# Spreading a memory's reciprocal norms over the partitions: matmuls of ones with a diagonal, or a DMA round trip over DRAM

## The chip, the core and the metric

The kernel runs on one core of one Trainium2 chip. The metric is device microseconds of one execution, the lower the better. The core has TensorE (PE in the profile; its weight loads are PEld), VectorE (DVE), ScalarE (ACT), GpSimd (POOL) and SyncE (SP), which issues nearly all DMAs; each engine runs its own queue of instructions in order.

## The reference, cut to what matters

The program is four blocks on 256 tokens of width 1024: an attention layer with global, windowed and memory heads, a layer with neighborhood and memory heads, a mixer, and a cross attention followed by a squared-ReLU MLP. Two of them read a memory, a [256, 1024] tensor that is normalised per token and projected to keys and values:

```python
memn = rmsnorm(mem, mem_norm_gain)
...
mk, mv = jnp.split(memn @ w_mem_kv[l], 2, axis=-1)
...
s = jnp.einsum('bshd,bmhd->bhsm', q, mk).astype(jnp.float32) * (dm ** -0.5)
...
kv = mem_n @ w_kv_mem
k, v = jnp.split(kv, 2, axis=-1)
```

The norm's factor is one number r per memory token. The kernel leaves it out of the projections and multiplies it in afterwards. Values come out with tokens on partitions, so r is a [128, 2] column there; keys come out transposed, with tokens along the free axis, so r is wanted as a [128, 256] tile that is alike in every partition.

## The kernel before, in words

Every weight matrix is streamed from DRAM in loads of up to 1 MB into one of three buffers of the tag `raw` (`load`, line 408). ScalarE copies a half of a load to `wh`, VectorE subtracts that from the load to get `wl` (`split`, line 413), and TensorE multiplies with three matmuls per product (hi by hi, hi by lo, lo by hi). A `raw` buffer is free once both of its halves are split. PSUM has two tags of four banks: `mm` for projections and `at` for everything of attention (`psum`, line 317). The softmax exponentials read the scores straight from their `at` bank (`softmax`, line 703), so a bank comes free only when ScalarE has run them. Attention steps are queued as background work between the pieces of weights (`later`, `pace`).

The order on each engine is not the order of the source. `Plan` (line 30) records all operations, takes a modelled cost for each (`cost`, line 131) and lists them by start with a list scheduler (`order`, line 162); then they are issued in that order, fixed, on each engine. Among the modelled figures: a POOL `pow` on [128, 2] takes 630 ns, and a DMA that isn't a weight load also waits, in the plan, for the matmul recorded before it (line 109).

`memory` (line 546) prepares a memory in background steps: squares of the two halves (`t_memraw`), then `finish`: `rstd` (line 500: one VectorE addition, one POOL `pow`), a VectorE copy to `t_memr`, and `spread` (line 491). It is called twice, for `mem` in the first layer and for `mem_2` in the second. `spread` writes the 256 numbers to DRAM (`t_rd`) and reads them back for all 128 partitions (`t_rb`), both on SyncE's queue, in which the weight loads stand too:

```python
nc.sync.dma_start(d.rearrange("(t p) -> p t", p=P), r)
b = self.base.tile([P, S], F32, name=self.name("rb"))
nc.sync.dma_start(b, d.rearrange("(o s) -> o s", o=1).to_broadcast([P, S]))
```

The only reader of `t_rb` is `mem_key` (line 577), which scales the keys. `layer_even` (line 954) already needs such a tile for the first input norm and makes it without DRAM (lines 982 to 988): VectorE scales the identity's columns by r to a diagonal, TensorE multiplies a [128, 128] tile of ones with it into an `at` bank, ScalarE copies the bank to SBUF.

Of the kernel before, what the change touches and what calls it, by code (L numbers as in the profile page):

```python
# [10 lines left out]
F32 = mybir.dt.float32  # L11
# [5 lines left out]
P = 128  # L17
S = 256
# [11 lines left out]
class Plan:  # L30
    """Records the program as operations on stand-ins of the tiles, then issues them in an order that keeps every
    dependence and the number of buffers of each tag, and that a list scheduler finds from the engines' costs."""
# [30 lines left out]
    def box(self, v):  # L63
        """the tile, the range of partitions and the set of elements in a partition, as bits, of an access"""
        t = self.tiles[v.tensor.name]
        if t["pool"].space == bass.MemoryType.DRAM:
            return t, (0, 1, 1)
        p0, f0 = divmod(v.offset, t["row"])
        if t["pool"].space == bass.MemoryType.PSUM:
            return t, (p0, p0 + v.ap[0][1], 1)  # L70
        bits = 1
        for step, num in sorted(list(v.ap)[1:], key=lambda d: abs(d[0])):
            if step < 0:
                f0 += step * (num - 1)
            if abs(step) == 1 and bits == 1:
                bits = (1 << num) - 1
            elif step:
                one = bits
                for k in range(1, num):
                    bits |= one << (abs(step) * k)  # L80
        return t, (p0, p0 + v.ap[0][1], bits << f0)
# [33 lines left out]
    def either(self, first, second):  # L115
        """an operation that one of two engines may run: each an engine, a method, its arguments and keywords"""
        self.record(*first)
        op = self.ops[-1]
        engine, method, args, kwargs = second
        out = args[0] if args else kwargs["out"]  # L120
        op["forms"].append((engine, method, args, kwargs, self.cost(engine, method, args, kwargs, [out], [args[1] if args else kwargs["in0"]])[0]))
        for j in op["deps"]:
            op["deps"][j] = max(op["deps"][j], self.latency(self.ops[j]["engine"], engine))
# [7 lines left out]
    def cost(self, engine, method, args, kwargs, outs, ins):  # L131
        """ns that the engine is held, ns until the result is there after that, bytes of a DMA"""
# [28 lines left out]
    # ------------------------------------------------------------------ order  # L161
    def order(self, prio):
        """a schedule: the operations by start, their starts and ends, and who held each back"""
# [104 lines left out]
    # ------------------------------------------------------------------ issue  # L268
# [18 lines left out]
class Kernel:  # L287
# [38 lines left out]
    # ------------------------------------------------- attention steps between the pieces of weights  # L326
# [18 lines left out]
    # ---------------------------------------------------------------- constants  # L345
# [61 lines left out]
    # ---------------------------------------------------------------- weights  # L407
# [19 lines left out]
    def proj_t(self, w, c0, hT, n=256, tag="mm"):  # L427
        """n (128 or 256) columns of h @ w, transposed: [128 columns, n / 128, 256 tokens] in one bank"""
        raw = self.load(w, 0, KT, c0, n)
        po = self.psum(tag)  # L430
        for f in range(n // P):
            wh, wl = self.split(raw[:, :, f * P:(f + 1) * P])
            for k in range(KT):
                self.mm3(po[:, f, :], wh[:, k, :], wl[:, k, :], hT(0, k), hT(1, k), k == 0, k == KT - 1)
                if k % 4 == 3:
                    self.pace()
        return po[:, :n // P, :]

    def proj_n(self, pieces, nk, n, hT, banks=None, start=True, stop=True):
        """h @ w for n columns in natural layout, a bank per token tile; pieces yields (first k tile, raw view)"""  # L440
# [16 lines left out]
    def wide(self, w, r0, nk, c0, n=512, step=4):  # L457
        """pieces of nk k-tiles by n columns, for proj_n; step k-tiles to a load"""
# [6 lines left out]
    # ---------------------------------------------------------------- norms  # L465
    def square_sums(self, src, c, ms):
        """ms[:, c, t] = the part of half c, src [P, 2, 512], in the mean of the squares over D"""
        for t in range(2):
            self.square_sum(src[:, t, :], ms[:, c, t:t + 1])

    def load_t(self, src, name):
        """[D, S] -> two tiles of 4 k-tiles"""
# [5 lines left out]
    def gain_t(self, src, key):  # L478
        """hi and lo of the tiles src with the gain: f(l, k) -> [P, S], and the step that fills k"""
# [11 lines left out]
    def spread(self, r):  # L491
        """[P, 2] per token -> [P, S], alike in every partition"""
        nc = self.nc
        d = self.dr.tile([S], F32, name=self.name("rd"))
        nc.sync.dma_start(d.rearrange("(t p) -> p t", p=P), r)
        b = self.base.tile([P, S], F32, name=self.name("rb"))
        nc.sync.dma_start(b, d.rearrange("(o s) -> o s", o=1).to_broadcast([P, S]))
        return b

    def rstd(self, ms):  # L500
        """ms [P, 2 parts, 2] -> [P, 2]"""
# [6 lines left out]
    def norm_twice(self, tag, gain, key, idle):  # L508
        """x = rmsnorm(x) * gain, and norm_later of that. Returns (after, go): after(c) for each half c of
        x once it is complete, then go() queues the steps and returns as turns"""  # L510
# [35 lines left out]
    def memory(self, tag, src, src_t, key, bias):  # L546
        """(src * gain).T, its hi and lo, and the rstd of src per token in both layouts, as attributes of a list
        filled in steps"""
# [12 lines left out]
        def finish():  # L561
            nc.vector.tensor_copy(r, self.rstd(ms))
            m[2] = self.spread(r)
# [13 lines left out]
    def mem_key(self, h, l, po, m):  # L577
        """hi and lo of po [P, 2, S] scaled per token"""
# [4 lines left out]
    def norm_later(self, tag, key, ms, idle):  # L583
        """rmsnorm(x).T in steps, the turning idle steps after the scaling"""
# [14 lines left out]
    def scaled(self, out, src, r):  # L599
        """out = src * r, r per partition"""  # L600
# [3 lines left out]
    def square_sum(self, v, ms):  # L604
        """ms = the part of v, [P, 512], in the mean of the squares over D"""
# [6 lines left out]
    def turns(self, tag, halves, key):  # L612
        """steps that fill hi and lo of (halves * gain).T; returns f(l, k) -> [P, S]"""
# [24 lines left out]
    # ---------------------------------------------------------------- evacuations  # L638
# [8 lines left out]
    def q_stack(self, po, scale):  # L647
        """[P, 2 pairs, S] of head pairs -> [P, 4 heads, S]; each head's rows hold its hi and lo parts"""
# [10 lines left out]
    def k_stack(self, po, pairs=2):  # L659
        """[P, pairs, S] of head pairs -> hi, lo [P, heads, S], both halves of the rows alike"""  # L660
# [15 lines left out]
    def v_heads(self, po):  # L676
        """two banks [P keys, 512] of 8 heads -> f(h)(k) -> [P, 128]: hi and lo of a head side by side"""
# [5 lines left out]
    # ---------------------------------------------------------------- attention  # L683
    def scores_stacked(self, q, kh, kl, spans):
        """spans: per query tile (first key, number of keys)"""
# [8 lines left out]
    def scores_full(self, parts):  # L694
        """parts: list of (qh, ql, kh, kl), each [P, S], summed over the list"""
# [7 lines left out]
    def softmax(self, sc, bias=None, sink=None, causal=False):  # L703
        """unnormalised weights and the reciprocals of their sums. With a bias, scores and bias are both
        negated."""
# [25 lines left out]
    def weights(self, p, rinv, causal=False):  # L731
        """normalised weights, transposed: hi, lo [P keys, 2, S queries]"""
# [16 lines left out]
    def pv_pair(self, ws, vs, causal=False):  # L749
        """o.T of two heads, [P, S]; vs: functions of the key tile giving a head's [P, 128] stationary, whose hi  # L750
        and lo columns give two halves of rows to be added"""
# [15 lines left out]
    def gate_tile(self, w, c0, hT):  # L767
        """2 * silu(h @ w[:, c0:c0+512]).T, [P, 4, S]"""
# [19 lines left out]
    def out_proj(self, w, r0, y, scale=None, after=None):  # L788
        """x += y @ w[r0:r0+512] (times a factor per token)"""
# [13 lines left out]
    def sums(self):  # L803
        """(ms, f): f(c) adds half c of x to ms once it is complete"""
# [10 lines left out]
    def filling(self):  # L815
        """projections of the second memory, as work for the tensor engine while it would wait"""
# [39 lines left out]
    def steps(self, tag, first, second, third, n, every):  # L856
        """queue the three steps of each of n heads, each step some steps behind the one before it; the third
        comes once for every heads"""
# [10 lines left out]
    def mem_heads(self, tag, qm, mk, mv, out):  # L869
        """steps of the four memory heads; out(h, o.T)"""  # L870
# [18 lines left out]
    def pair_heads(self, tag, n, scores, bias, sink, v, out, causal=False):  # L889
        """steps of n heads in pairs: scores(h), bias(h), sink(h), v(h)(l, k), out(pair, o.T)"""  # L890
# [14 lines left out]
    # ---------------------------------------------------------------- layers  # L905
    def rope(self, tag, po, n, i, rx):
        """steps of per-head rmsnorm and rotation of n heads of 64; po: a bank per token tile, still to be
        scaled by rx; returns the list that they fill"""
# [45 lines left out]
    def layer_even(self):  # L954
# [27 lines left out]
        diag = self.work("p", [P, 2, P], PB)  # L982
        pb = self.psum("at")
        rb = self.work("y", [P, S], YB)
        for t in range(2):
            nc.vector.tensor_scalar(diag[:, t, :], self.ident, r[:, t:t + 1], None, ALU.mult)
            nc.tensor.matmul(pb[:, 0, t * P:(t + 1) * P], self.ones, diag[:, t, :], start=True, stop=True)
        nc.scalar.copy(rb, pb[:, 0, :])
# [78 lines left out]
    def heads8(self, tag, w_in, cq, ck, cv, hT, bias, out, causal=False, before=None):  # L1067
        """8 heads of 64; the scores come out negated"""
# [76 lines left out]
    def token_rms(self, sq):  # L1145
        """sq [P, 4, S]: squares, of 4 feature tiles, over their number -> rstd [P, 2] per token"""
# [306 lines left out]
```

## Time and profile before

| what | before |
|---|---|
| time, median of 3 runs (lowest to highest) | 796.77 us (792.59 to 798.28) |
| profiled execution: span from first to last instruction | 790.9 us |
| profiled execution: its own time with what lies around the span | not reported |
| TensorE busy | 771.2 us of the span |
| VectorE, ScalarE, POOL busy | 576.7, 505.3, 74.4 us |
| moved by DMA | 140.85 MB, mean 178 GB/s |

Every operation is issued from one line of `Plan.issue`, so all rows carry L284 and are told apart by their tiles: `t_wh<-t_raw` is a split on ScalarE, `t_at<-t_ks,t_qs` are scores, `t_p<-t_at,t_st` an exponential, `t_mm<-t_gh,t_wh` a projection of a memory. A line of the waits gives the engine that stood, what released it, total us, times and the longest. The chain of waits is followed back from the last instruction, each step to what released it. An fp32 matmul shows as two records here.

### The profile page before, as it was taken

How to read it: one execution, taken by the hardware profiler on the slowest of the kernel's cores; microseconds unless marked ns; L12 is line 12 of the kernel's file. 1: busy time of each engine (PE TensorE's matmuls, PEld its weight loads, DVE VectorE, ACT ScalarE, POOL GpSimd, SP SyncE). 2: the span in 40 equal slices, each digit the busy share in tenths (PEclk: the TensorE clock that was granted, in tenths of full speed). 3: DMA queues.
4: the chain of work that ended last, by engine and by line, in shares of the span. 5: the costliest groups of instructions: out<-in, count | busy, mean ns of one | idle time of the engine just before them, and what ended most of it. 6: DMA issues, size and time to landing. Idle time of an engine off the chain costs nothing.

```text
span 790.9 us, 13554 instructions
## 1 busy us (share of the span) xinstructions
PE 771.2 (98%) x5312; PEld 716.6 (91%) x5312; DVE 576.7 (73%) x991; ACT 505.3 (64%) x926; POOL 74.4 (9%) x105
## 2 busy tenths in 40 slices
PE   8997999999999999999999999999999999999996
PEld 7797899889899989997999899899989999999985
DVE  6996987997768759879987788975667544545444
ACT  6784966875658559648786777475456654555452
POOL 0640000000001420232011100100000000000000
PEclk9999999999999999999999999999999999999999
DMA  7794546345558785684457735356434555565631
GB/s 229 253 319 149 169 136 220 126 142 163 183 168 275 193 189 167 187 226 146 147 166 196 224 115 163 123 188 227 152 128 161 183 189 186 187 195 179 201 119 53
DMA packets 110827, 140.85 MB, mean 178 GB/s; under 512 B 4355, under 2 KB 82371, under 8 KB 110764
## 3 DMA queue, kind: packets, MB, share of 16 engines
q1 hardware_dynamic: 105292, 131.90, 51.3%
q0 software_dynamic: 5472, 8.10, 4.8%
q8 instruction: 41, 0.67, 0.4%
q14 instruction: 22, 0.18, 0.1%
HBM read 135.25 MB, written 1.07 MB: 172 GB/s over the span
## 4 chain that ended last, share of the span: by engine, by line
PE 85%; DVE 5%; DMA 5%; POOL 2%; issue 2%; ACT 1%; SPq 0%; POOLq 0%; ACTq 0%; DVEq 0%
PE t_mm L284 63%; PE t_at L284 22%; DVE t_wl L284 2%; DMA t_rd<-t_memr 2%; DMA t_raw<-in_w_mem_kv_dram 1%; DMA t_raw<-in_w_out_odd_dram 1%; DVE t_y L284 1%; POOL t_rrs L284 1%; DVE t_p L284 1%; ACT t_wh L284 1%; POOL t_ks L284 1%; DMA t_raw<-in_w_in_even_dram 1%; DVE t_xs L284 0%; POOL t_rstd L284 0%; ACT t_p L284 0%
## 5 line engine op out<-in xcount | busy, mean ns | idle before, releaser
L284 DVE TENSOR_TENSOR t_wl<-t_raw,t_wh 128x1024 fp32r<-128x1024 f32 (+1 forms) x237 | 290.1, 1228 | 147.4 <-ACT t_wh L284 146.9
L284 ACT ACTIVATE t_wh<-t_raw 128x1024 fp32r<-128x1024 f32 (+1 forms) x237 | 248.9, 1054 | 207.0 <-PE t_mm L284 136.0
L284 PE MATMUL t_mm<-t_mT,t_wh 128*128 128x256 f32 x992 | 192.4, 287 | 0.0
L284 PEld LDWEIGHTS t_mm<-t_mT,t_wh 128*128 128x128 f32 x992 | 159.4, 191 | 0.4
L284 PE MATMUL t_mm<-t_mT,t_wl 128*128 128x256 f32 x496 | 141.1, 285 | 0.0
L284 PE MATMUL t_mm<-t_wh,t_yh 128*128 128x512 f32 x288 | 113.7, 395 | 0.0
L284 PE MATMUL t_mm<-t_wl,t_yh 128*128 128x512 f32 x288 | 113.6, 395 | 0.0
L284 PE MATMUL t_mm<-t_wh,t_yl 128*128 128x512 f32 x288 | 113.1, 394 | 0.0
L284 PE MATMUL t_at<-t_mT,t_wh 128*128 128x256 f32 x480 | 97.0, 282 | 0.0
L284 PEld LDWEIGHTS t_mm<-t_mT,t_wl 128*128 128x128 f32 x496 | 95.0, 192 | 0.0
L284 PEld LDWEIGHTS t_at<-t_mT,t_wh 128*128 128x128 f32 x480 | 78.8, 190 | 1.6
L284 PE MATMUL t_mm<-t_wh,t_gh 128*128 128x256 f32 (+2 forms) x256 | 66.0, 340 | 1.7 <-ACT t_wh L284 1.7
L284 PE MATMUL t_at<-t_mT,t_wl 128*128 128x256 f32 x240 | 67.6, 282 | 0.0
L284 PE MATMUL t_mm<-t_hT,t_wh 128*128 128x256 f32 x336 | 66.2, 287 | 0.2 <-ACT t_wh L284 0.2
L284 PEld LDWEIGHTS t_mm<-t_wh,t_yl 128*128 128x128 f32 x288 | 54.2, 188 | 10.7
L284 PEld LDWEIGHTS t_mm<-t_wl,t_yh 128*128 128x128 f32 x288 | 54.2, 188 | 10.0
L284 PEld LDWEIGHTS t_mm<-t_wh,t_yh 128*128 128x128 f32 x288 | 54.2, 188 | 9.7
L284 ACT ACTIVATE t_p<-t_p,t_st 128x256 f32<-128x256 f32 (+1 forms) x118 | 55.8, 490 | 7.6 <-DVE t_st L284 7.4
L284 POOL TENSOR_TENSOR t_rstd<-t_rstd,t_mhalf 128x2 f32<-128x2 f32 (+1 forms) x12 | 12.2, 1015 | 477.1 <-DVE t_rstd L284 477.1
L284 PEld LDWEIGHTS t_mm<-t_hT,t_wh 128*128 128x128 f32 x336 | 54.1, 191 | 0.5 <-ACT t_wh L284 0.4
L284 PE MATMUL t_mm<-t_gh,t_wh 128*128 128x256 f32 x256 | 51.6, 290 | 0.0
L284 PEld LDWEIGHTS t_mm<-t_wh,t_gh 128*128 128x128 f32 x256 | 44.6, 193 | 6.3 <-ACT t_wh L284 1.9
(171 smaller groups left out, 1318.0 us busy)
## 6 DMA issues: line engine op xcount, KB each, us to landing
t_raw<-in_w_in_odd_dram SPq DMA_DIRECT2D x20, 1024.0 KB, 5.2
t_raw<-in_w_up_dram SPq DMA_DIRECT2D x16, 1024.0 KB, 5.4
t_raw<-in_w_down_dram SPq DMA_DIRECT2D x16, 1024.0 KB, 4.9
t_raw<-in_w_in_dram SPq DMA_DIRECT2D x12, 1024.0 KB, 5.2
t_raw<-in_w_in_even_dram SPq DMA_DIRECT2D x10, 1024.0 KB, 5.0
t_raw<-in_w_mem_kv_dram SPq DMA_DIRECT2D x8, 1024.0 KB, 8.3
t_raw<-in_w_out_even_dram SPq DMA_DIRECT2D x6, 1024.0 KB, 5.0
t_raw<-in_w_out_odd_dram SPq DMA_DIRECT2D x6, 1024.0 KB, 5.8
```

What stands on the lines that cost most here:

```text
L284: f(*[self.real(v) for v in args], **{k: self.real(v) for k, v in kwargs.items()})
```

## The change

`spread` takes the tile to fill as an argument and makes it with the chain that `layer_even` had inline; `layer_even` calls it, with the same tiles as before, and `memory` calls it for both memories. The DRAM tile and the two DMAs per memory are gone. The plan is made anew from the changed list of operations. The rest of the diff empties docstrings and comments.

```diff
-    def spread(self, r):
...
-        nc = self.nc
-        d = self.dr.tile([S], F32, name=self.name("rd"))
-        nc.sync.dma_start(d.rearrange("(t p) -> p t", p=P), r)
-        b = self.base.tile([P, S], F32, name=self.name("rb"))
-        nc.sync.dma_start(b, d.rearrange("(o s) -> o s", o=1).to_broadcast([P, S]))
+    def spread(self, r, b):
+
+        nc = self.nc
+        diag = self.work("p", [P, 2, P], PB)
+        pb = self.psum("at")
+        for t in range(2):
+            nc.vector.tensor_scalar(diag[:, t, :], self.ident, r[:, t:t + 1], None, ALU.mult)
+            nc.tensor.matmul(pb[:, 0, t * P:(t + 1) * P], self.ones, diag[:, t, :], start=True, stop=True)
+        nc.scalar.copy(b, pb[:, 0, :])
         return b
...
             nc.vector.tensor_copy(r, self.rstd(ms))
-            m[2] = self.spread(r)
+            m[2] = self.spread(r, self.base.tile([P, S], F32, name=self.name("rb")))
...
         r = self.token_rms(sq[0])
-        diag = self.work("p", [P, 2, P], PB)
-        pb = self.psum("at")
-        rb = self.work("y", [P, S], YB)
-        for t in range(2):
-            nc.vector.tensor_scalar(diag[:, t, :], self.ident, r[:, t:t + 1], None, ALU.mult)
-            nc.tensor.matmul(pb[:, 0, t * P:(t + 1) * P], self.ones, diag[:, t, :], start=True, stop=True)
-        nc.scalar.copy(rb, pb[:, 0, :])
+        rb = self.spread(r, self.work("y", [P, S], YB))
```

## Rows read from the trace of the kernel before

**Rows 1.** The page, part 1 (busy time, share of the span and number of instructions of each engine) and the granted clock of TensorE in 40 equal slices of part 2.

```profile
PE 771.2 (98%) x5312; PEld 716.6 (91%) x5312; DVE 576.7 (73%) x991; ACT 505.3 (64%) x926; POOL 74.4 (9%) x105
...
PEclk9999999999999999999999999999999999999999
```

**Rows 2.** Who waited for whom, the waits of TensorE's own queue, longest first. Columns: engine and tile that waited, arrow, what released it, then us in total, times, longest us.

```profile
PE t_at L284 <- ACT t_p L284: 4.8, 1, 4.8
PE t_mm L284 <- ACT t_wh L284: 1.9, 2, 1.7
PE t_at L284 <- DVE t_st L284: 1.8, 1, 1.8
PE t_at L284 <- DVE t_p L284: 1.6, 3, 1.0
```

**Rows 3.** The chain of waits that ended last, in the stretch 44 to 84 us. Columns: start us, us, what.

```profile
59.98 11.10 DMA t_raw<-in_w_mem_kv_dram
...
71.16 1.06 ACT t_wh L284
72.22 1.83 ACT t_p L284 x8
...
74.09 1.22 PE t_at L284 x4
```

**Rows 4.** Instructions of TensorE in order of time, 64 to 83 us. Columns: start us, us, engine, line, operation, out<-in, shape, count, and in brackets the idle time before and its releaser.

```profile
69.05 0.28 PE L284 MATMUL t_mm<-t_gh,t_wh 128*128 128x256 f32 x1
74.09 1.22 PE L284 MATMUL t_at<-t_ks,t_qs 128*128 128x256 f32 x4 [4.76 <-ACT t_p L284]
```

**Rows 5.** Busy time of each engine (PE, PEld, DVE, ACT, POOL) in stretches of 2 us, then granted clock, share of the DMA engines and GB/s.

```profile
74.00:76.00 2.00, 1.91 (x9) 1.91 (x10) 2.00 (x5) 2.00 (x8) 0.00 (x0) 0.50 0.03 12
76.00:78.00 2.00, 2.00 (x14) 2.00 (x14) 2.00 (x3) 1.06 (x3) 0.00 (x0) 0.74 0.52 147
```

**Rows 6.** Issues on SyncE's queue in order of time, 18 to 100 us. Columns as in the group of TensorE's instructions above.

```profile
57.68 0.37 SPq L284 DMA_DIRECT2D t_rd<-t_memr  x1
59.98 0.37 SPq L284 DMA_DIRECT2D t_raw<-in_w_mem_kv_dram  x1
66.41 0.34 SPq L284 DMA_DIRECT2D t_rb<-t_rd  x1
```

**Rows 7.** DMA queues in the stretch 58 to 66.4 us: packets of all queues, then issues with size and us from issue to landing.

```profile
DMA packets 417, 0.23 MB, mean 28 GB/s; under 512 B 277, under 2 KB 346, under 8 KB 416
...
t_raw<-in_w_mem_kv_dram SPq DMA_DIRECT2D x1, 1024.0 KB, 11.1
t_rd<-t_memr SPq DMA_DIRECT2D x1, 1.0 KB, 8.7
```

**Rows 8.** The page, part 6, issues over the whole span. Columns: out<-in, queue, operation, count, KB each, median us to landing.

```profile
t_raw<-in_w_in_odd_dram SPq DMA_DIRECT2D x20, 1024.0 KB, 5.2
...
t_raw<-in_w_mem_kv_dram SPq DMA_DIRECT2D x8, 1024.0 KB, 8.3
...
t_raw<-in_w_out_odd_dram SPq DMA_DIRECT2D x6, 1024.0 KB, 5.8
```

**Rows 9.** Instructions of ScalarE in order of time, 50 to 86 us.

```profile
71.16 1.06 ACT L284 ACTIVATE t_wh<-t_raw 128x1024 fp32r<-128x1024 f32 x1 [6.79 <-DMA t_raw<-in_w_mem_kv_dram]
```

**Rows 10.** The chain of waits in the stretch 255 to 300 us.

```profile
267.92 12.49 DMA t_rd<-t_memr
...
280.87 8.36 DMA t_raw<-in_w_out_odd_dram
...
292.45 0.74 PE t_at L284 x4
```

**Rows 11.** SyncE's waits over the whole span, those on the first DMA of the round trip.

```profile
SPq L284 <- DMA t_rd<-t_memr: 17.9, 2, 11.9
```

**Rows 12.** Instructions of VectorE, 262 to 294 us.

```profile
271.77 1.23 DVE L284 TENSOR_TENSOR t_wl<-t_raw,t_wh 128x1024 fp32r<-128x1024 f32 x1 [1.49 <-ACT t_wh L284]
...
290.42 1.23 DVE L284 TENSOR_TENSOR t_wl<-t_raw,t_wh 128x1024 fp32r<-128x1024 f32 x1 [4.11 <-ACT t_wh L284]
```

**Rows 13.** Instructions of all engines in the first layer, 18 to 26 us, where the same chain of ones and diagonal already stands.

```profile
20.41 0.39 PE L284 MATMUL t_mm<-t_wh,t_gh 128*128 128x512 f32 x1
...
20.78 0.55 DVE L284 TENSOR_SCALAR t_p<-t_cst,t_rstd 128x128 f32<-128x128 f32 x2 [0.59 <-POOL t_rstd L284]
...
21.17 0.71 PE L284 MATMUL t_at<-t_p,t_ones 128*128 128x128 f32 x4 [0.37 <-DVE t_p L284]
...
21.64 0.48 PE L284 MATMUL t_mm<-t_wh,t_gh 128*128 128x512 f32 x1
...
22.14 0.36 ACT L284 COPY t_y<-t_at 128x256 f32<-128x256 f32 x1
```

**Rows 14.** VectorE's instructions around the two places, 50 to 86 us and then 244 to 254 us (two answers of one view).

```profile
55.57 0.16 DVE L284 SCALAR_TENSOR_TENSOR t_rstd<-t_ms 128x2 f32<-128x2 f32 x1
...
57.48 0.17 DVE L284 COPY t_memr<-t_rstd 128x2 f32<-128x2 f32 x1 [0.61 <-POOL t_rstd L284]
...
73.16 0.17 DVE L284 RECIPROCAL t_st<-t_st 128x2 f32<-128x2 f32 x1 [5.29 <-ACT t_p L284]
...
244.45 0.15 DVE L284 SCALAR_TENSOR_TENSOR t_rstd<-t_ms 128x2 f32<-128x2 f32 x1
...
250.04 0.16 DVE L284 COPY t_memr<-t_rstd 128x2 f32<-128x2 f32 x1
```

## The prediction

> **What bounds the kernel now.** I read the page's busy times first. TensorE is busy for 771.2 of 790.9 us, at nine tenths or more of the clock in every slice [rows 1], so a gain can only come from the 19.7 us in which it stands, or from its clock. Next come TensorE's own waits: the longest, 4.8 us, ends with an exponential on ScalarE, and another, 1.8 us, with a softmax statistic on VectorE [rows 2]. The chain of waits tells what was late behind each.
>
> At the first place the chain goes from a weight load of the memory's projections that took 11.10 us, over its split on ScalarE, over eight pieces of exponentials, to score matmuls at 74.09 [rows 3]. TensorE started its last projection matmul at 69.05 and stood for 4.76 us [rows 4], because the scores want an `at` bank, the bank comes free with an exponential, and ScalarE, whose queue has the split ahead of it, waited 6.79 us for the load [rows 9]. After that standstill the granted clock is 0.50 in 74 to 76 and 0.74 in 76 to 78 us [rows 5], that is time at 1.2 in place of 2.4 GHz. The load was issued at 59.98, behind the 1 KB write of the round trip (57.68), and SyncE came on only at 66.41 with the read back [rows 6]. That write took 8.7 us to land, and from 58 to 66.4 us all queues together moved 0.23 MB, 28 GB/s [rows 7]. So the 1 MB load stood behind a transfer of 1 KB on an otherwise nearly empty fabric.
>
> At the second place the chain names the write itself: 12.49 us, then a load of `w_out_odd` of 8.36 us, a split, scores at 292.45 [rows 10]. Here SyncE's queue was blocked: it waited 11.9 us for the write, 17.9 us over both places [rows 11].
>
> **Removed.** *First place.* Without the write, the load of 59.98 lands after the 5.2 us that loads of this size usually take [rows 8], at 65.2. Its split (1.06) and the exponentials (1.83) [rows 3] end at 68.1, before TensorE runs out at 69.3; the wait of 4.8 us goes. Bounds: loads of this one matrix have a median of 8.3 us [rows 8]; landing at 68.3, with the 3.0 us from landing to scores as now (71.08 to 74.09 [rows 3]), the scores would start at 71.3 and 2.0 of the wait would stay. I take 5.2, since what was in flight beside it is the write that goes. With the standstill goes the slow clock: 74.09 to 76 at half speed costs 0.95 us and 76 to 78 at 0.74 another 0.5 [rows 4, 5], together 1.5. What is late next is the second half of the keys' split, which VectorE does right after the exponentials; it has 2 to 3 us of other matmuls ahead of it. ScalarE's 6.79 us and VectorE's 5.29 us of idle time [rows 9, 14] go with TensorE's, so the attention work behind moves up by as much as TensorE does.
>
> A rule of the Trainium skill speaks against this term. DMA: Bandwidth & Descriptors, in the section on the anatomy of one DMA, gives a transfer (one that GpSimd issues) a fixed 2.0 us and little more than its bytes; by that estimate the write would land by 59.7, and the load issued at 59.98 could not have been late because of it. The traced 8.7 and 12.49 us disagree. By the rule the term is 0, by the rows 4.8 plus the clock.
>
> *Second place.* The buffer for the late load was free when the split begun at 271.77 ended, 273.00 [rows 12]; the load was issued at 280.87 [rows 10]. It moves up 7.9 us and lands, with the matrix's median of 5.8 [rows 8], at 278.8; ScalarE wanted it near 284, VectorE's idle 4.11 us starts later still [rows 12]. The 1.8 us go; bounds 0 and 1.8. The granted clock there needs no term.
>
> SyncE also saves four issues, about 0.4 us each [rows 6]; nothing but loads waits there, so that is inside the terms.
>
> **Added.** The first layer already runs the same chain [rows 13]. *TensorE:* two fp32 matmuls, four records, hold the queue from 21.17 to the next matmul at 21.64, 0.47 us. Ahead of them it stood 0.37 us for VectorE's diagonal, 0.84 together. Bounds per place: 0.47 where nothing is waited for, and above what the rival below gives. I take 1.0 twice, a little over the nearest row, because at both places VectorE is late with the copy ahead of the diagonal: 57.48, released by POOL, and 250.04, 5.6 us after the addition [rows 14]. That is 2.0 us on the path, since TensorE is the bound. Behind the waiting matmul stands all of TensorE's queue: projections, then scores, and ScalarE's splits wait for those.
>
> *VectorE:* two diagonals, 0.55 us per place; *ScalarE:* one copy, 0.36 us [rows 13]. Both cost nothing where the engines now idle (6.79, 5.29 and 4.11 us [rows 9, 12, 14]); without that cover 1.8 us in all. I take 0: after the change these engines come free earlier than now by more than that.
>
> *Buffers:* the chain takes one of four `at` banks and one of four `p` tiles from its matmul to its copy. If all were wanted then, a score would be late by one exponential, 0.46 us (1.83 for eight pieces, two to each of two tiles [rows 3]). I take 0: at the first place TensorE has projections to run until 69.
>
> **Sum.** 4.8 + 1.8 + 1.5 - 2.0 = 6.1 us off the span of 790.9. The time of the profiled execution is not shown; its span lies 5.9 us under the median of 796.77, and I carry the difference to that median: 790.7 us. With no wait at the new matmuls 4.8 + 1.8 + 1.5 - 0.9 = 7.2, or 789.6. With the slower landing (2.0 us of wait stay, clock kept) 4.1, or 792.7.
>
> **Rivals.**
>
> *The load is late anyway.* The write's packets and the load's may have nothing to do with each other, and the fabric was slow for another reason. Then only the second place gains: 1.8 - 2.0 = -0.2, 797.0 us. For it: the median of 8.3 us for this matrix, with other loads around it. Against it: at the second place the write took as long by itself, with SyncE's queue blocked and no load behind it [rows 10, 11]. The Trainium skill stands with this rival: the same page says, on queues, rings and completion order, that data descriptors carry no barrier, so a later transfer may finish ahead of an earlier one. No row here shows two transfers overtaking. Chance 0.11.
>
> *TensorE waits at the new matmuls.* The plan takes 630 ns for the POOL `pow`; at the first place addition to copy took 1.9 us, at the second 5.6 [rows 14]. If the plan puts the matmul where it thinks the diagonal is ready, and TensorE gets there on time, it stands for up to those spans and the diagonals: 1.9 + 5.6 + 2 x 0.55 = 8.6 us, with a slow clock after it like the one at 74 us, 1.5, and 0.9 of matmuls: 11.0 against the 8.1 gained, 2.9 slower, 799.7 us. It decides once the waits together pass 7.2 us. For it: TensorE's queue is in order and had no such wait at these places. Against it: VectorE's order comes from the same plan, so the 5.6 us are mostly planned; and in the whole trace TensorE stood for VectorE's `t_p`, the same kind of feed, 1.6 us in three times [rows 2]. Chance 0.12; half of that passes the slower bound, if the later standstill pushes further loads.
>
> *The new order is better elsewhere too.* The planner starts afresh from two fewer DMAs per memory. If the small waits go that are left, 1.9 and 1.6 us [rows 2], the gain is 9.6, 787.2 us. Against it: nothing ties those waits to the round trip, and an equal number could appear. Chance 0.15.
>
> *The change does nothing* can't be: the DMAs sit on the chain of waits at both places.
>
> **Numbers.** The forecast, 790.7, has 0.62. About 1%, 8 us, is what can be told from no change: below 788.8 is faster, above 804.7 slower. The forecast stays inside, but the three runs before scatter from 4.2 below to 1.5 above their median, so of its 0.62 I give 0.12 to faster. Faster 0.12 + 0.15 = 0.27; slower 0.06; the rest, 0.67, is within. The range goes from 785.0 (789.6 less 4.2, rounded) to 797.0, the load that is late anyway; what lies outside is mostly the waiting TensorE.
>
> **What will show it.** In TensorE's waits the lines of 4.8 on ScalarE's `t_p` and 1.8 on VectorE's `t_st` are gone, and the granted clock near 75 us is 1.00 throughout. On SyncE no wait for a round trip is left, and loads of about 65 and 273 us follow the freeing of a buffer. New are four diagonals and four times two records of ones on TensorE; idle time ahead of them says whether the 1.0 us per place is right. I am wrong if the load issued near 60 us still takes 8 us or more, if TensorE stands several us at the new matmuls, or if a wait of this size turns up at a place that the change doesn't touch.

## The result and the profile after

The changed kernel takes 786.87 us (786.07 to 788.59 over four runs) against 795.87 us for the kernel before, run beside it: ratio 0.989, interval 0.9857 to 0.9923, so 1.1% or 9.0 us faster. The two profiled executions differ by less: 784.3 against 790.9 us of span, 6.6 us. Each run of the changed kernel lies 1.7 to 1.9 us above its own span. The page after, as [rows 1]:

```profile
PE 769.9 (98%) x5320; PEld 715.2 (91%) x5320; DVE 578.2 (74%) x995; ACT 506.3 (65%) x928; POOL 74.7 (10%) x105
```

TensorE has the eight records more that two diagonals per memory cost. Its own waits, as [rows 2]:

```profile
PE t_mm L284 <- ACT t_wh L284: 2.5, 1, 2.5
PE t_at L284 <- DVE t_p L284: 2.0, 4, 1.0
PE t_at L284 <- POOL t_warm L284: 1.3, 1, 1.3
PE t_at L284 <- DMA t_tanh<-in_onehot_dram: 0.8, 1, 0.8
PE t_mm L284 <- DVE t_wl L284: 0.6, 2, 0.4
```

The lines of 4.8 and 1.8 us are gone. The 2.5 us on `t_wh` belong to the start, at 7.68 us, where before had 1.7 of its 1.9; no other single wait is longer than 1.3 us. A fourth wait on `t_p` is the price of the first new chain. Issues on SyncE's queue, 44 to 82 and 255 to 300 us, as [rows 6]:

```profile
45.26 20.60 SPq L284 DMA_DIRECT2D t_raw<-in_w_mem_kv_dram  x4
70.65 6.81 SPq L284 DMA_DIRECT2D t_raw<-in_w_in_even_dram  x2
...
263.03 6.17 SPq L284 DMA_DIRECT2D t_raw<-in_w_out_odd_dram  x2
274.48 22.83 SPq L284 DMA_DIRECT2D t_raw<-in_w_in_odd_dram  x4
```

Four loads of the memory's weights go out by 65.86 us with nothing of the round trip between them. The load of `w_out_odd` that before issued at 280.87 [rows 10] is now the second of the two from 263.03, issued by 269.20: its buffer comes free with a split from 267.31 to 268.81, the counterpart of the one begun at 271.77 [rows 12], and SyncE is there to use it. The DMA queues from 58 to 66.4 us, as [rows 7]:

```profile
DMA packets 622, 1.15 MB, mean 137 GB/s; under 512 B 25, under 2 KB 109, under 8 KB 621
...
t_raw<-in_w_mem_kv_dram SPq DMA_DIRECT2D x2, 1024.0 KB, 5.1
```

The same 8.4 us now carry 1.15 MB in place of 0.23, and a load of this matrix takes 5.1 us in place of 11.1. ScalarE's split of it no longer waits for the load, and the granted clock stays at its upper level in the two stretches of [rows 5]:

```profile
74.00:76.00 2.00, 2.00 (x20) 2.00 (x19) 2.00 (x5) 2.00 (x4) 0.00 (x0) 1.00 0.54 185
76.00:78.00 2.00, 2.00 (x19) 2.00 (x18) 1.83 (x3) 2.00 (x8) 0.00 (x0) 1.00 0.00 0
```

The new chain in TensorE's order of time, first and second place, each with the matmul behind it (two answers of one view):

```profile
58.75 0.71 PE L284 MATMUL t_at<-t_p,t_ones 128*128 128x128 f32 x4 [0.49 <-DVE t_p L284]
59.22 0.36 PE L284 MATMUL t_mm<-t_hT,t_wh 128*128 128x256 f32 x1
...
254.35 0.61 PE L284 MATMUL t_at<-t_p,t_ones 128*128 128x128 f32 x4
254.71 0.49 PE L284 MATMUL t_mm<-t_mT,t_wh 128*128 128x256 f32 x2
```

At the first place it costs 0.49 us of standing and 0.47 until the next matmul (58.75 to 59.22), at the second 0.36 and nothing stood.

### The profile page after: what moved, and what is told of

Its sections match the earlier page's. It is cut to its first block, busy times and chain, and to the rows that moved or that the text cites. A ratio compares the mean times of both kernels' runs of the same rounds, so it can differ in the third digit from the quotient of the medians.

```text
span 784.3 us, 13568 instructions
## 1 busy us (share of the span) xinstructions
PE 769.9 (98%) x5320; PEld 715.2 (91%) x5320; DVE 578.2 (74%) x995; ACT 506.3 (65%) x928; POOL 74.7 (10%) x105
## 4 chain that ended last, share of the span: by engine, by line
PE 88%; DVE 4%; issue 3%; POOL 2%; DMA 1%; ACT 1%; SPq 0%; POOLq 0%; DVEq 0%; ACTq 0%
PE t_mm L284 66%; PE t_at L284 22%; DVE t_wl L284 1%; POOL t_rrs L284 1%; DMA t_xT<-in_x_t_dram 1%; DVE t_y L284 1%; DVE t_p L284 1%; POOL t_ks L284 1%; DMA t_tanh<-in_onehot_dram 0%; SPq L284 0%; ACT t_wh L284 0%; POOL t_rstd L284 0%; DVE t_gh L284 0%; DVE t_sq L284 0%; ACT t_tanh L284 0%
## 5 line engine op out<-in xcount | busy, mean ns | idle before, releaser
L284 PE MATMUL t_mm<-t_hT,t_wh 128*128 128x256 f32 x336 | 66.4, 287 | 0.0
```

What stands on the lines that cost most here:

```text
L284: f(*[self.real(v) for v in args], **{k: self.real(v) for k, v in kwargs.items()})
```

## The experiments

Three theories were to be told apart. **The write:** its 256 pieces of 4 bytes are slow to land and hold up the 1 MB loads issued beside it. **The queue:** the loads suffer from SyncE's queue, in which they stand behind the write and in which SyncE stands still until the read back. **The plan:** the round trip is innocent, and the new order happens to be better. The runs were made in three jobs, each with its own runs of the kernel before: 796.79, 798.12 and 796.5 us. Ratios are against those, each with its 95% interval; they are not the quotients of the two medians.

**One place at a time.** `memory` calls the new chain for one memory and the old round trip for the other, and an unchanged kernel before ran beside them:

```diff
-            m[2] = self.spread(r, self.base.tile([P, S], F32, name=self.name("rb")))
+            if tag == "mem":      # second_only: "mem2"
+                m[2] = self.spread(r, self.base.tile([P, S], F32, name=self.name("rb")))
+            else:
+                m[2] = self.round_trip(r)
```

> Matmuls for the first memory, the round trip kept for the second. Theory (the write of 1 KB holds what stands behind it on SyncE's queue): TensorE's wait of 4.8 on ScalarE's t_p is gone, the granted clock near 75 us is 1.00, the wait of 1.8 on VectorE's t_st stays; 4 to 6 us less than before, near 790. Rival (the load is late anyway): the 4.8 stays and the time is that of before within 1 us.

> The round trip kept for the first memory, matmuls for the second. Theory: the wait of 4.8 and the slow clock near 75 us stay, the wait of 1.8 is gone; 1 to 2 us less than before. Rival (the places are worth the same, since SyncE was blocked longer at the second): 3 us or more less than before.

> The unchanged kernel once more, to see why the medians moved by 9.0 us while the two profiled spans differ by 6.6. Theory (the scatter of the kernel before is the length of the standstill near 70 us, and the profiled execution was its shortest): spans between 791 and 797, time 1.5 to 2 us above each span, and TensorE's wait on ScalarE's t_p longer than 4.8 in a longer execution. Rival (the scatter has to do with nothing in the kernel): the same wait of 4.8 within 0.5 us, and the rest of a longer span spread over other places.

Measured: first_only 788.01 us (0.9882, 0.9832 to 0.9933), second_only 792.04 (0.9944, 0.9919 to 0.9969), before_again 793.08 (0.9944, 0.9918 to 0.997). TensorE's waits of first_only hold no exponential any more, but part of the second place's:

```profile
PE t_at L284 <- DVE t_st L284: 0.7, 1, 0.7
```

and second_only is its mirror, with the first standstill whole and the second gone:

```profile
PE t_at L284 <- ACT t_p L284: 4.5, 1, 4.5
```

Against before_again in the same job, the first place is worth 5.1 us and the second 1.0. That before_again, the same program as its reference, came out 3.7 us shorter than it is a warning: two loadings of this kernel can differ by more than the second place is worth. Against 796.79 us, the other loading of before in the same job, first_only is 8.8 us less and second_only 4.8, as the rival of second_only had it, and the two together are more than the whole change gained. I go by before_again, and by the traces, in which each of the two kernels lacks the wait of its own place. To see how far loadings differ, I ran the kernel before a third time, beside the changed kernel.

**Like for like.** before_third is the kernel before unchanged, after_again the changed kernel unchanged, in one job.

> The unchanged kernel a third time, beside the changed one. The second time its ratio to the same code was 0.9944 [0.9918, 0.997]. Theory (two loadings of one program differ in how long the loads near 60 us take, so in how often the clock falls): again off the kernel before by up to 4 us either way, longer spans with a lower mean clock. Rival (a property of the comparison): again 3 to 4 us less.

> The changed kernel beside the unchanged one of this job. Theory: 6 to 7 us less than the unchanged kernel when that has the spans it had the second time (793), 9 or more when it has those of the kernel before (797); its own spans scatter by less than 3 us, since the standstill with its clock is gone.

Measured: 796.75 us (0.9995, 0.9967 to 1.0024) and 785.91 (0.9879, 0.9848 to 0.991): 10.8 us apart. The spans of the before_third runs reach from 789.5 us at a mean granted clock of 0.993 to 797.5 at 0.987; those of after_again lie between 783.5 and 785.8, at 0.996 to 0.999. The waits of before_third's profiled execution, span 794.6 us:

```profile
PE t_at L284 <- ACT t_p L284: 5.1, 1, 5.1
PE t_at L284 <- DVE t_st L284: 2.4, 1, 2.4
```

and its stretches of 2 us (columns as in [rows 5]), around both standstills:

```profile
74.00:76.00 2.00, 1.50 (x7) 1.50 (x8) 2.00 (x4) 2.00 (x8) 0.00 (x0) 0.50 0.11 41
76.00:78.00 2.00, 2.00 (x11) 2.00 (x10) 2.00 (x5) 1.46 (x4) 0.00 (x0) 0.50 0.25 84
78.00:80.00 2.00, 2.00 (x12) 2.00 (x10) 0.51 (x1) 0.19 (x1) 0.00 (x0) 0.50 1.07 378
...
294.00:296.00 2.00, 1.34 (x6) 1.25 (x7) 2.00 (x11) 2.00 (x7) 1.92 (x3) 0.78 1.10 346
296.00:298.00 2.00, 2.00 (x6) 1.52 (x6) 2.00 (x7) 1.97 (x8) 1.76 (x2) 0.50 1.04 330
298.00:300.00 2.00, 2.00 (x11) 1.63 (x10) 1.44 (x4) 0.25 (x1) 0.00 (x0) 0.87 0.20 69
```

The granted clock is the column behind POOL's. After the first standstill TensorE works 5.5 us at 1.2 GHz (1.5 in the first stretch and two whole ones), which costs 2.75 us; the execution before the change had lost 1.5 there. The second standstill is followed by a slow stretch as well, some 1.7 us (the shares 0.22, 0.50 and 0.13 that are missing from three times 2 us), where the profile of before showed none. With 5.1 and 2.4 us of waits that makes 12.0; less the new chain's 1.3 us (0.49 + 0.47 + 0.36), 10.7, and the two profiled spans, 794.6 and 784.2, differ by 10.4.

**The write or the queue.** write_kept is the changed kernel with the old write put back for both memories. Nothing reads it, so SyncE never stands for it. pool_queue is the kernel before with both DMAs of `spread` on GpSimd's queue, so that no weight load stands behind either.

```diff
 # write_kept, after the changed spread
+            d = self.dr.tile([S], F32, name=self.name("rd"))
+            nc.sync.dma_start(d.rearrange("(t p) -> p t", p=P), r)
 # pool_queue, in the spread of before
-        nc.sync.dma_start(d.rearrange("(t p) -> p t", p=P), r)
+        nc.gpsimd.dma_start(d.rearrange("(t p) -> p t", p=P), r)
-        nc.sync.dma_start(b, d.rearrange("(o s) -> o s", o=1).to_broadcast([P, S]))
+        nc.gpsimd.dma_start(b, d.rearrange("(o s) -> o s", o=1).to_broadcast([P, S]))
```

> The changed kernel with the 1 KB write added back for both memories; nobody reads what it writes and nobody waits for it. Theory (the write itself holds the loads behind it): the write again takes 8 us or more to land, a load issued within a few us behind it takes 8 to 11 us, TensorE stands again 2 to 5 us near 70; 3 to 6 us more than the changed kernel. Rival (only SyncE's wait for the write did harm, the load of 60 us was late for another reason): time of the changed kernel within 1 us, loads behind the write land in 5 to 6 us.

> The kernel before with both DMAs of the round trip issued on GpSimd's queue. Theory A (the harm is done on SyncE's queue, by what the write holds there and by the wait for it): both waits, 4.8 and 1.8, are gone, 6 to 8 us less than before, no new matmuls. Theory B (the write slows all DMA engines, whichever queue it came from): the load near 60 us still takes 8 us or more and the 4.8 stays, only the 1.8 goes; 1 to 2 us less than before.

Measured: write_kept 792.54 us (0.9935, 0.9913 to 0.9956), 5.7 above the changed kernel's 786.87, which is of another job; by the two ratios it is 3.6. In its trace every engine has the instructions of the changed kernel in the same order, by operation and tile, with nothing more than the two writes on SyncE. Its DMA queues, 58 to 66.4 us:

```profile
DMA packets 563, 0.34 MB, mean 41 GB/s; under 512 B 288, under 2 KB 517, under 8 KB 562
...
t_raw<-in_w_mem_kv_dram SPq DMA_DIRECT2D x2, 1024.0 KB, 10.7
t_rd<-t_memr SPq DMA_DIRECT2D x1, 1.0 KB, 8.3
```

A write whose result nobody wants doubles the time of the load. TensorE's wait for the exponential is back at 3.4 us, and the granted clock is 0.50 from 74 to 80 us. The stretches (DMA share and GB/s are the last two columns) show when the load, issued at 61.07, begins to move:

```profile
62.00:64.00 2.00, 2.00 (x19) 2.00 (x18) 2.00 (x4) 0.69 (x1) 0.00 (x0) 1.00 0.08 20
64.00:66.00 2.00, 2.00 (x19) 2.00 (x19) 2.00 (x4) 1.44 (x2) 0.00 (x0) 1.00 0.38 28
66.00:68.00 2.00, 2.00 (x19) 2.00 (x18) 1.90 (x5) 0.11 (x1) 0.00 (x0) 1.00 0.37 43
68.00:70.00 2.00, 2.00 (x19) 2.00 (x18) 1.76 (x3) 0.00 (x0) 0.00 (x0) 1.00 0.85 279
```

The write lands at 66.7 (58.39 + 8.3). The load's bytes run after that, so it isn't slowed by sharing bandwidth: it hardly moves while the write is in flight. Nor is it the moving of the pieces that takes the time. The packets of all queues from 58.2 to 60.5 us, and from 60.5 to 62 us:

```profile
DMA packets 446, 0.16 MB, mean 71 GB/s; under 512 B 288, under 2 KB 446, under 8 KB 446
...
DMA packets 0, 0.00 MB, mean 0 GB/s; under 512 B 0, under 2 KB 0, under 8 KB 0
```

The small pieces (288 packets under 512 bytes, 256 of them the write's; write_rows, with 128 pieces, has 160 there) have gone by 60.5 us, before the load behind them is issued, and for 1.5 us nothing moves at all; the landing comes at 66.7. So the load is not what makes the write late. The second place of the kernel before shows the same: from 274 to 276 us no packet moves on any queue, from 276 to 280 only 16, none of them under 512 bytes, and the write issued at 267.92 lands at 280.41.

pool_queue 794.52 us (0.9973, 0.9948 to 0.9998), its waits and, from the DMA queues of the same 8.4 us, the write:

```profile
PE t_at L284 <- ACT t_p L284: 6.0, 1, 6.0
...
PE t_at L284 <- DVE t_st L284: 0.4, 1, 0.4
```

```profile
t_raw<-in_w_mem_kv_dram SPq DMA_DIRECT2D x2, 1024.0 KB, 11.4
t_rd<-t_memr POOLq DMA_DIRECT2D x1, 1.0 KB, 8.9
```

On another queue the write is as slow and harms the load of the first place as much; of the two loads whose median is 11.4, the one issued at 59.58 took 12.35 us. The second place got better, 0.4 us, since SyncE no longer stands for the write; TensorE, VectorE and ScalarE have the order of before in this trace, instruction for instruction. So the write explains the first place, the standing queue the second, and the new order neither: write_kept has the new order and the first stall again, and pool_queue has the old order and nearly none of the second. In six executions with the old write the load lands its usual time after the write has landed, whichever queue carries the write:

| kernel | write lands | load lands | between |
|---|---|---|---|
| before | 57.68 + 8.7 = 66.38 | 59.98 + 11.10 = 71.08 | 4.7 us |
| before_again | 57.33 + 8.7 = 66.03 | 59.62 + 11.88 = 71.50 | 5.5 us |
| second_only | 58.58 + 8.2 = 66.78 | 60.88 + 10.84 = 71.72 | 4.9 us |
| write_kept | 58.39 + 8.3 = 66.69 | 61.07 + 10.67 = 71.74 | 5.1 us |
| before_third | 57.79 + 8.8 = 66.59 | 60.09 + 11.39 = 71.48 | 4.9 us |
| pool_queue | 57.55 + 8.9 = 66.45 | 59.58 + 12.35 = 71.93 | 5.5 us |

**What of the write is slow.** The same dead write of 1 KB, laid out in two other ways: write_rows gives each partition's two numbers one stretch of 8 bytes (128 pieces); write_lines keeps 256 pieces of 4 bytes but puts each into 64 bytes of DRAM of its own.

```diff
 # write_rows
+            nc.sync.dma_start(d.rearrange("(p t) -> p t", p=P), r)
 # write_lines
+            d = self.dr.tile([S, 16], F32, name=self.name("rd"))
+            nc.sync.dma_start(bass.AP(d.tensor, d.offset, [[16, P], [16 * P, 2]]), r)
```

> The changed kernel with a dead write of the same 1 KB whose DRAM side is laid out so that each partition's two numbers lie side by side. Theory (the number of small packets makes the write slow): half as many packets, landing about half as late as in the kernel with the write kept, less harm or none. Rival (any write of small packets to DRAM lands this late): landing as there, within 1.5 us.

> As the kernel with the write kept, 256 packets of 4 bytes, but each number to its own 64 bytes of DRAM. The write with 128 packets of 8 bytes landed after 3.1 us, that with 256 of 4 bytes side by side after 8.3. Theory A (packets of 4 bytes into the same stretch of DRAM wait for one another): lands in 3 to 4 us and TensorE doesn't stand near 70. Theory B (the count of packets or their size): lands in 7 to 9 us, TensorE stands again 2 to 6 us, 3 to 6 us more than the changed kernel.

Measured: write_rows 786.0 us (0.9853, 0.9807 to 0.99), write_lines 786.98 (0.9886, 0.9849 to 0.9924): both as the changed kernel, with no wait for the exponential and the granted clock at 1.00 from 70 to 82 us. The DMA queues of write_rows, 58 to 66.4 us:

```profile
t_raw<-in_w_mem_kv_dram SPq DMA_DIRECT2D x2, 1024.0 KB, 6.4
t_rd<-t_memr SPq DMA_DIRECT2D x1, 1.0 KB, 3.1
```

and of write_lines, 55 to 62 us:

```profile
t_raw<-in_w_mem_kv_dram SPq DMA_DIRECT2D x1, 1024.0 KB, 5.0
t_rd<-t_memr SPq DMA_DIRECT2D x1, 1.0 KB, 2.1
```

In the traces write_kept, write_rows and write_lines have the same instructions in the same order on every engine, so the layout of a write that nobody reads decides by itself whether TensorE stands for the exponential. With as many pieces as before, as small as before, the write lands in 2.1 us when its pieces are 64 bytes apart, and in 8.2 to 8.9 side by side. So neither the number nor the size of the pieces makes it slow by itself. Lying side by side doesn't do it alone either: write_rows has half as many pieces of twice the size, without a gap, and lands in 3.1. Nor is the gap all that write_lines changes: its pieces cover 16 KB of DRAM in place of 1 KB. Which of these counts was not taken further apart. In both kernels the write had landed (61.7 and 59.3 us) by about the time the load was issued (61.30 and 59.88), and the load took 6.4 and 5.0 us. They show that a short write does little harm or none, not that a long one with this layout would be harmless.

**The price of the chain.** chain_twice runs it twice per memory into the same tile. early_finish leaves the chain single and lets the planner put it, and the `pow` and copy ahead of it, earlier; early_again is the same file, run beside after_again.

```diff
 # chain_twice
-            m[2] = self.spread(r, self.base.tile([P, S], F32, name=self.name("rb")))
+            b = self.base.tile([P, S], F32, name=self.name("rb"))
+            self.spread(r, b)
+            m[2] = self.spread(r, b)
 # early_finish, early_again
+            nc.bias = -400
             nc.vector.tensor_copy(r, self.rstd(ms))
             m[2] = self.spread(r, self.base.tile([P, S], F32, name=self.name("rb")))
+            nc.bias = 0
```

> The changed kernel with the chain of diagonal, ones and copy run twice for each memory, the first result overwritten. It measures what the chain costs. By the prediction's term, 1.0 us per place: 2.0 more than the changed kernel. By the changed kernel's trace, 0.47 of matmuls per place and a wait of 0.5 at the first only: 0.9 to 1.2 more.

> The changed kernel with the planner's priority of the addition, pow, copy and chain raised by 400 places, so that the diagonal no longer comes late behind POOL. Theory: the waits of 0.5 and of what stands beside it near 58 us go, 0.5 to 1.2 us less than the changed kernel. Rival (the order moves other work into TensorE's way): no gain or a loss of up to 2 us.

> The changed kernel with the chain's priority raised, in one job with the changed kernel. Theory: 0.5 to 1.5 us less than the changed kernel, as the medians 785.39 and 786.87 of two jobs say. Rival: no difference beyond 0.5 us.

Measured: chain_twice 787.08 us (0.9871, 0.9839 to 0.9904), early_finish 785.39 (0.9852, 0.9819 to 0.9885), early_again 784.77 (0.9864, 0.9834 to 0.9893). In its own job early_again is 1.14 us below after_again, and the two sets of runs (784.42 to 785.3, 785.31 to 787.7) touch but don't overlap; by its median it is the fastest version here. Its wait on the diagonal is gone, where after has 2.0 in four times:

```profile
PE t_at L284 <- DVE t_p L284: 1.4, 3, 1.0
```

chain_twice lies 1.69 above early_finish in one job; with the 1.14 of the other job, a second chain at both places costs an estimated 0.55 us in all, less than the 2.0 or the 0.9 to 1.2 expected. The gain of 1.14 is more than the 0.5 us of wait that it removes; where the rest comes from was not followed.

## Why the prediction was right, and where it was off

I said 790.7 us, within a range of 785.0 to 797.0; 786.87 lies in it, and I gave faster by over 1% only 0.27. The mechanism at both places was right in the main, and the gain in span came out near the forecast. That the range holds the median is in part luck: its lower end is the forecast without waits less 4.2 us, the scatter of three runs, and not the bound of any step. The steps:

*The first wait of 4.8 us and what caused it: right in effect, half right in cause.* I wrote that the load "stood behind a transfer of 1 KB". It did wait for it: with the write gone it takes 5.1 us, with the write back, 10.7. But it isn't that it stood behind the write on SyncE's queue: on GpSimd's queue the write does the same. The rival with a load that is late anyway is thereby excluded; write_kept decides against it.

My argument against that rival, that at the second place the write took as long by itself, was read too simply: another load, issued 0.42 us ahead of the write, and other transfers moved beside it until 274 us; the write landed 6.4 us after that.

The Trainium skill, DMA: Bandwidth & Descriptors, puts a fixed 2.0 us on a transfer that GpSimd issues (anatomy of one DMA): SyncE's write with 64 bytes to each piece landed in 2.1 us, but the same bytes side by side took four times as long, 8.9 us where GpSimd issued them. The specifications on that page say that transfers under 512 bytes make the engine read, modify and write. That is so for the quick layouts as well as for the slow one, and no run here shows whether it plays a part: the traces end with the pieces gone by 60.5 us, and what happens until the landing, and why the loads' bytes wait for it, stays open.

*The second place, 1.8 us: right.* SyncE's blocking was the cause, as [rows 10, 11] had it: pool_queue, without it, is down to 0.4, write_kept, which has the write but no wait for it, shows no such wait, and with the new chain it is gone. The size varies with the execution: 1.8, 1.5 and 2.4 us in three profiles of before, with 0.7 in first_only.

*The clock, 1.5 us: this term was too small.* I read one slow stretch from one execution and gave the second place none. Others show half rate from 72 or 74 to 78 or 80 us, and before_third a further one near 296: 2.75 + 1.7 = 4.4 us. So the stall's length (4.5 to 6.0 us with the round trip at this place) and its price in clock both change from run to run, and the profiled execution was a cheap one.

*From span to median, 5.9 us: wrong in kind.* I took the distance between the span and the median for what lies around a span. That is 1.7 to 1.9 us in each run of the changed kernel and in most runs of before, with up to 3.3 in some. By that the profiled execution of before took 790.9 + 1.7 to 3.3 us, which fits only its shortest run, 792.59 us, and the median was long because other executions lost more in standstills and clock. The change removes that as well. So the spans' forecast of 6.1 us off was close to the 6.6 measured, and the carry is what failed: the gain between medians was 9.0 in place of 6.1. That is 2.9 of the 3.8 us by which the forecast is too high; the other 0.9 is the median of before itself, 795.87 beside the changed kernel in place of 796.77. The part of the mean clock is to be seen in the ranges: 0.987 to 0.996 in runs of before, 0.995 to 0.999 in the changed kernel's.

*The chain, 1.0 us per place: right at the first (0.96), too dear at the second (0.36).* The copy ahead of the diagonal was again 5.6 us behind the addition (239.54 to 245.13), and TensorE never noticed: the diagonal is made at 247.33, the matmul stands at 254.35. That is against the rival in which TensorE waits at the new matmuls; of it there are 0.49 us. VectorE's 0.47 us of diagonals and ScalarE's copy, 0.38 us, cost nothing that could be told from none, as forecast.

*The new order is better elsewhere.* This rival's figure, 787.2, is nearest to the median, but not for its reason: the small waits that it wanted gone, on `t_p` and `t_wh`, are still there as 2.0 and 2.5 us.

What stays open is why one loading of the unchanged program ran 3.7 us below another in the same job (0.9944, 0.9918 to 0.997); against it the changed kernel's two medians, both of other jobs, are 6.2 and 7.2 us less, where beside the kernel before the change was worth 9.0 and 10.8.

## What to carry to other kernels

When a load is late on a nearly idle fabric, look at what else was in flight from its issue to its landing, on every queue: a 1 KB transfer can cost a megabyte load 5 us, and moving it to another queue doesn't help. If scratch in DRAM can't be avoided, try small pieces with space between them, or one longer piece from each partition (only the write was measured so, not a read back from such a layout); better, keep a column of 256 numbers on chip, at 0.4 to 1.0 us of TensorE. Price a standstill by several executions and with the clock that follows it, and don't carry a difference between one profiled span and a median of runs as if it were overhead.

## What was not expected of the hardware

One kilobyte written to DRAM lands in 2.1, 3.1 or 8.2 to 8.9 us at the first place by its layout alone, and in 10.8 (pool_queue) to 12.6 (before_third) at the second in the old layout, where other transfers run beside its first half. The time is not in moving the pieces: in write_kept they have gone 6.2 us before the write lands. And a load on one queue is late with a write on another: in pool_queue it landed 5.5 us after the write on GpSimd's did, though it had been issued 6.9 us before that (59.58 and 66.45).
